# Batches of four adaLN units, gated rows shifted by 64 bytes, and two orders of the split products, in a hybrid decoder step

## The chip, the cores and the metric

One core of a Trainium2 chip. The metric is the device time of one execution in microseconds (us): the median of three runs. The engines are TensorE (PE, with its weight loads as PEld), VectorE (DVE), ScalarE (ACT), GpSimd (POOL) and SyncE (SP, which only issues DMAs here).

## The reference, cut to what matters

One inference step of a two-layer trunk over 512 prompt tokens and 64 sample tokens (576 columns, eight samples of eight tokens), width 1024, float32. Each layer is a half SwiGLU, a mixer, and a second half SwiGLU:

```
cs = silu(c)
for l in range(2):
    mod = cs @ ada_w[l] + ada_b[l]                  # nine blocks of 1024
    sh1, sc1, g1, sh2, sc2, g2, sh3, sc3, g3 = split(mod, 9)
    h = rms_norm(x, g) * (1 + sc1) + sh1
    x = x + 0.5 * g1 * ((silu(h @ w_gate) * (h @ w_up)) @ w_down)   # inner width 2816
    h = rms_norm(x, g) * (1 + sc2) + sh2
    x = x + g2 * mixer(h)            # l = 0: GLA and gMLP heads; l = 1: mLSTM
    ...                              # a second SwiGLU with sh3, sc3, g3
y = rms_norm(x, g) * (1 + scf) + shf
```

So there are four feed-forward sub-layers, called (0,0), (0,1), (1,0) and (1,1) here, in the order (0,0), mixer 0, (0,1), (1,0), mixer 1, (1,1), final norm. The product `cs @ ada_w`, with only nine rows of `cs`, is the adaLN work.

## The kernel before, in words

Activations lie with features on the 128 partitions and the 576 tokens along the row. Every dense product is made in three parts: weights and activations are split into a high part (rounded to fp32r) and a low part (the rest), and PE makes high x high, high x low and low x high (`tile3`). The 576 columns are two halves of 288, whose sums lie in two PSUM banks, so one tile of 128 x 128 weights costs six matmuls of 288 columns: three products times two halves, each with a weight load of its own. `dense` runs eight such tiles (k) into one PSUM buffer: 48 matmuls. `self.turn` picks the order of the six: "products" (both halves of one product, then the next), "halves" (three products of one half, then of the other), "serpent" (the second product's halves the other way round) or "low" (the third product before the second). `ffn` sets one of these for each of the four feed-forwards and "products" everywhere else:

```
self.turn = {(0, 0): "halves", (0, 1): "serpent", (1, 0): "low", (1, 1): "products"}[l, i]
```

A feed-forward works in three groups of 8, 7 and 7 blocks of the inner width. For each block j: a gate product (`pg`), silu on ACT, an up product (`pu`), their product on DVE, and the split of that into `hh` and `hl`, the gated rows. The first gate and up of a sub-layer are made together (`dense_pair`), as the norm hands out its rows k by k. Then eight down products (m) run over the group's `hh` and `hl`: 8 x 8 x 6 = 384 matmuls in the first group, 336 in each other. Group by group, gate and up are 768 matmuls in the first (96 of them the pair) and 672 in each other.

The weights come through SP in units of up to 512 KB (`w_load`, three buffers) and are split by ACT and DVE some three pieces ahead (`w_split`).

The adaLN product is cut into 80 tiles of 128 x 2048 (1 MB each) in ten groups of eight. A "unit" is one step of `ada_gen`: units 0 to 7 of a group issue four matmuls on 32 of PE's columns each (the trace shows eight instructions, as float32 takes two), a ninth step copies the sums to SBUF (`adasb`), a tenth transposes them and makes shift, scale and gate (`mod`). `fill(n)` takes n steps; (0,0) and (0,1) have 20 to take: one behind each gate product and one behind each up product until they are used up. `finish`, at a sub-layer's end, takes one step, the last row sums of squares, and seven more, while the next norm starts on DVE and ACT. `ada_dma` loads tiles up to six ahead into seven buffers.

SBUF is given out by pools, as a stack: a pool that is opened lies above those that are open, and what was closed is used again. Inside a pool, buffers lie in order of first use. `reuse_waits="tile"` lets a new tile wait for the last reader of each old tile whose bytes it takes. In a feed-forward two pools are opened: `room()` is the adaLN pool (`adasb` 2048 bytes a partition, `mod` 576, and seven `adaw` buffers of 8192), `hp` holds `hh`, `hl` (2304 bytes each) and small tiles. In (0,0) `room()` comes first, in the other three `hp`. In (0,1) and (1,0) the first use is of `adasb` and `mod`, then of `adaw`. A pool's first `adaw` tile goes into the lowest buffer; in (1,0) the next ones go from the top downwards; from the eighth tile on the buffers repeat in the same order. The weights `whi` and `wlo` start at multiples of 128 bytes, the normed rows `xh` and `xl` as well. `hh` and `hl` start 64 bytes past such a multiple in (0,0), as 7 x 8192 + 2048 + 576 = 59968 = 468 x 128 + 64, and at a multiple in the other three.

The norm of the next sub-layer opens its pool (`rstd` 2304 bytes, four `yn` buffers of 2304) when both are closed: for (1,0) at the byte where the pools of (0,1) started, for mixer 1 33408 bytes above the byte where those of (1,0) started. In front of some places a `spare` tile keeps `adaw` buffers clear of the next norm.

Of the kernel before, what the change touches and what calls it, by code (L numbers as in the profile page):

```python
# [98 lines left out]
def all_units():  # L99
    yield from ffn_units(0, 0)  # L100
    yield from ab_units()
    yield from ffn_units(0, 1)
    yield from ffn_units(1, 0)
    yield from ml_units()
    yield from ffn_units(1, 1)
# [22 lines left out]
class Trunk:  # L128
    def __init__(self, ctx, tc, ins, outs):
        self.tc, self.nc, self.ins, self.outs = tc, tc.nc, ins, outs  # L130
        pool = lambda name, bufs=1, **kw: ctx.enter_context(tc.tile_pool(name=name, bufs=bufs, **kw))
        self.const = pool("const")
        self.wp = pool("wp", 2)
        self.work = pool("work", 2)
        self.psd = pool("psd", 2, space=PSUM)
        self.psc = pool("psc", 3, space=PSUM)
        self.psa = pool("psa", 1, space=PSUM)
        c = self.const
        self.x = c.tile([P, KD, T], F32, name="x")
        self.sh = c.tile([P, 7, KD, NC], F32, name="sh")  # L140
        self.am = c.tile([P, 7, KD, NC], F32, name="am")
        self.gm = c.tile([P, 6, KD, NC], F32, name="gm")
        self.adab = c.tile([P, 160], F32, name="adab")
        self.gn = c.tile([P, 7, KD], F32, name="gn")
        self.ones = c.tile([P, P], F32, name="ones")
        self.ident = c.tile([P, P], F32, name="ident")
        self.eps = c.tile([P, 1], F32, name="eps")
        self.cs = c.tile([P, KD, 32], F32, name="cs")

        self.units, self.pieces, off = [], [], 0  # L150
        for u, (n, _) in enumerate(all_units()):
            self.units.append((off, n))
            off += P * n
            self.pieces += [(u, c0, min(512, n - c0)) for c0 in range(0, n, 512)]
        self.n_load = self.n_split = self.n_piece = 0
        self.raw, self.split = {}, {}

        self.ada_load = 0
        self.ada_tiles = {}
        self.ada = self.ada_gen()  # L160
        self.ada_done = self.ada_step = 0
        self.ada_ahead = 0
        self.queue = []
        self.cut = HT
        self.turn = "products"


    def w_load(self, upto):
# [30 lines left out]
    def tile3(self, ps, wh, wl, xh, xl, start, stop):  # L199

        mm = self.nc.tensor.matmul
        c = self.cut
        parts = [(slice(512 - c, 512), slice(0, c)), (slice(512, 512 + T - c), slice(c, T))]
        products = ((wh, xh), (wh, xl), (wl, xh))
        turns = {"products": [(j, a) for j in range(3) for a in range(2)],
                 "halves": [(j, a) for a in range(2) for j in range(3)],
                 "serpent": [(0, 0), (0, 1), (1, 1), (1, 0), (2, 0), (2, 1)],
                 "low": [(j, a) for j in (0, 2, 1) for a in range(2)]}[self.turn]
        seen = [0, 0]
        for j, a in turns:  # L210
            w, xx = products[j]
            o, t = parts[a]
            seen[a] += 1
            mm(ps[:w.shape[1], o], w, xx[:, t], start=start and seen[a] == 1, stop=stop and seen[a] == 3)  # L214

    def psum(self):

# [89 lines left out]
    def fill(self, n):  # L307
        for _ in range(n):
            if next(self.ada, 0) == 0:
                return  # L310
            self.ada_step += 1

    def fill_mm(self, n):

        while n and self.ada_step % 10 < 8:
            self.fill(1)
            n -= 1
# [138 lines left out]
    def ffn(self, l, i, ss, fills, gap):  # L456
        nc = self.nc
        left = fills
        s = l * 3 + 2 * i
        if s:  # L460
            self.norm(s, ss, mid=self.split_next)
        else:
            self.first_norm(ss)
        with ExitStack() as ctx:
            room = lambda: self.ada_pool(ctx, f"ada{l}{i}", 7, 8 * gap)
            if s == 0:
                room()
            hp = ctx.enter_context(self.phase(f"hp{l}{i}"))
            if s:
                room()  # L470
            xs = self.xk()
            self.turn = {(0, 0): "halves", (0, 1): "serpent", (1, 0): "low", (1, 1): "products"}[l, i]
            f0 = 0
            for gi, n in enumerate(FGROUPS):
                hh = [hp.tile([P, T], F32R, name=f"hh{j}", tag=f"hh{j}") for j in range(n)]
                hl = [hp.tile([P, T], F32R, name=f"hl{j}", tag=f"hl{j}") for j in range(n)]
                for j in range(n):
                    if gi == 0 and j == 0:
                        pg, pu = self.dense_pair(xs, KS)
                        if self.ada_step % 10 == 8:  # L480
                            self.fill(2)
                        if fills:
                            self.ada_prefetch()
                    else:
                        pg = self.dense(xs, KS)
                    sg = hp.tile([P, T], F32, name="sg", tag="sg", bufs=2)
                    nc.scalar.activation(sg, pg, AF.Silu)  # L487
                    if gi or j:
                        n_fill = min(left, 1)
                        self.fill(n_fill)  # L490
                        left -= n_fill
                        pu = self.dense(xs, KS)
                    h = hp.tile([P, T], F32, name="h", tag="h", bufs=2)
                    nc.vector.tensor_tensor(out=h, in0=sg, in1=pu, op=ALU.mult)  # L494
                    self.hilo(h, hh[j], hl[j])
                    if gi or j:
                        n_fill = min(left, 1)
                        self.fill(n_fill)
                        left -= n_fill
                last = gi == len(FGROUPS) - 1  # L500
                if last:
                    self.log_exp()
                    ss = self.ss_tiles()
                for m in range(KD):
                    ps = self.dense((hh, hl), range(n))
                    if last and m:
                        self.sumsq(m - 1, ss)
                    self.x_add(m, ps, self.gm[:, s])
                    if last and not fills:
                        self.ada_dma(min(self.ada_load + 1, self.ada_stop))  # L510
                f0 += n
            self.turn = "products"
            self.finish(ss)
        return ss

# [1156 lines left out]
```

## Time and profile before

| | |
|---|---|
| median of three runs | 2802.16 us (2801.65 to 2807.85) |
| profiled execution, its time | 2799.31 us |
| its span, first to last instruction | 2797.5 us |
| PE busy | 2722.1 us of the span, 97% |
| PEld, DVE, ACT, POOL busy | 2457.4, 1264.6, 839.3, 193.6 us |
| mean granted PE clock | 0.987 |
| PE in the chain that ended last | 90%, of which 74% is line 214, the matmul of `tile3` |

A row of the timeline gives an instruction's start, how long it took, engine, line, operation, what it writes and reads, its shape, and how many were merged. Matmuls overlap: a 288-column one takes 0.29 us from start to end, but the next starts some 0.13 us after it, so stretches are read from start to start. A row of windows gives the stretch, its length, the busy time and (in brackets) the number of instructions by engine, the granted clock, the mean busy share of the DMA engines, and GB/s.

### The profile page before, as it was taken

Reading aid. Unit: us, or ns where it says so; the run is one execution under the profiler, and the core shown is the slowest. Engines: PE = TensorE matmul, PEld = TensorE weight load, DVE = VectorE, ACT = ScalarE, POOL = GpSimd, SP = SyncE. Lnnn points to the kernel's source line nnn. Section 1 sums busy time; section 2 is a strip of 40 time slices with the busy share of each in tenths; the row PEclk is TensorE's granted clock in tenths of the full one; section 3 lists DMA queues with packets and bytes.
Section 4 is the critical chain, followed back from the end, with each engine's and each line's share of the span. In section 5 each row is a group of like instructions: output and inputs, shape, how many; then the busy total and the mean of one; then the engine's idle time right before and its main releaser. Section 6 shows DMA issues by size and latency. Waiting matters only on the chain.

```text
span 2797.5 us, 45631 instructions
## 1 busy us (share of the span) xinstructions
PE 2722.1 (97%) x19182; PEld 2457.4 (88%) x19182; DVE 1264.6 (45%) x2442; ACT 839.3 (30%) x1508; POOL 193.6 (7%) x263
## 2 busy tenths in 40 slices
PE   6999999999999999999999999999999999999997
PEld 4899999787788999998999997999577667999997
DVE  4233334456552333345333336654766776333334
ACT  4222223332242222234222234334323324222223
POOL 1000000022110000001000004310100111000000
PEclk9999999999799999999999999999999999999999
DMA  7533223221147442223222234467875665222222
GB/s 288 212 126 136 84 82 116 90 77 39 37 168 271 136 138 81 85 84 113 83 84 80 87 126 171 151 179 237 317 280 208 258 250 198 84 83 82 84 76 73
DMA packets 114741, 388.49 MB, mean 139 GB/s; under 512 B 19417, under 2 KB 37097, under 8 KB 95721
## 3 DMA queue, kind: packets, MB, share of 16 engines
q1 hardware_dynamic: 102088, 336.62, 35.7%
q0 software_dynamic: 4880, 35.06, 3.2%
q10 hardware_dynamic: 7568, 13.90, 1.3%
q8 instruction: 151, 2.47, 0.4%
q14 instruction: 54, 0.43, 0.0%
HBM read 324.95 MB, written 60.59 MB: 138 GB/s over the span
## 4 chain that ended last, share of the span: by engine, by line
PE 90%; DVE 4%; ACT 2%; issue 1%; DMA 1%; POOL 1%; SPq 0%; DVEq 0%; ACTq 0%; POOLq 0%
PE psd L214 74%; PE psd L555 2%; PE psc L1509 2%; PE psa L274 1%; PE psc L1397 1%; PE psa L1480 1%; PE psc L1414 1%; PE psc L822 1%; DVE yn L381 1%; POOL qe L805 1%; PE psc L1363 1%; PE psd L1488 1%; DVE xl L371 1%; PE psd L1366 1%; PE psd L1367 0%
## 5 line engine op out<-in xcount | busy, mean ns | idle before, releaser
L214 PE MATMUL psd<-xh,whi 128*128 128x288 f32 x3648 | 852.7, 299 | 11.7 <-ACT xh L382 7.6
L214 PE MATMUL psd<-xl,whi 128*128 128x288 f32 x3648 | 842.9, 297 | 7.9 <-DVE xl L371 7.5
L214 PE MATMUL psd<-xh,wlo 128*128 128x288 f32 x3648 | 839.8, 296 | 1.5 <-DVE wlo L185 1.5
L185 DVE TENSOR_TENSOR wlo<-wraw,whi 128x512 fp32r<-128x512 f32 (+1 forms) x696 | 459.2, 698 | 455.2 <-ACT whi L184 450.9
L214 PEld LDWEIGHTS psd<-xh,whi 128*128 128x128 f32 x3648 | 607.9, 189 | 55.7 <-issue 18.1
L214 PEld LDWEIGHTS psd<-xl,whi 128*128 128x128 f32 x3648 | 608.1, 189 | 13.4 <-DVE xl L371 12.8
L214 PEld LDWEIGHTS psd<-xh,wlo 128*128 128x128 f32 x3648 | 607.7, 189 | 1.8 <-DVE wlo L185 1.8
L184 ACT CAST whi<-wraw 128x512 fp32r<-128x512 f32 (+1 forms) x696 | 400.1, 608 | 416.2 <-PE psd L214 376.0
L214 PE MATMUL psd<-hl,whi 128*128 128x288 f32 x1408 | 329.3, 295 | 0.0
L214 PE MATMUL psd<-hh,whi 128*128 128x288 f32 x1408 | 329.3, 295 | 0.0
L214 PE MATMUL psd<-hh,wlo 128*128 128x288 f32 x1408 | 329.2, 295 | 0.0
L428 DVE SCALAR_TENSOR_TENSOR x<-psd,gm,x 128x512 f32<-128x512 f32 x136 | 102.1, 750 | 355.6 <-PE psd L214 355.6
L214 PEld LDWEIGHTS psd<-hh,whi 128*128 128x128 f32 x1408 | 235.9, 188 | 1.7 <-issue 1.7
L214 PEld LDWEIGHTS psd<-hl,whi 128*128 128x128 f32 x1408 | 235.8, 188 | 0.0
L214 PEld LDWEIGHTS psd<-hh,wlo 128*128 128x128 f32 x1408 | 235.1, 188 | 0.0
L494 DVE TENSOR_TENSOR h<-sg,psd 128x576 f32<-128x576 f32 x88 | 66.4, 754 | 349.2 <-PE psd L214 349.2
L420 ACT CAST hh<-h 128x576 fp32r<-128x576 f32 x88 | 59.4, 675 | 488.4 <-DVE h L494 488.4
L487 ACT ACTIVATE sg<-psd 128x576 f32<-128x576 f32 x88 | 57.4, 652 | 359.4 <-PE psd L214 359.3
L367 POOL TENSOR_TENSOR yn<-x,rstd 128x576 f32<-128x576 f32 x30 | 49.3, 1651 | 1062.5 <-ACT rstd L395 1005.9
L214 PE MATMUL psd<-hz,whi 128*128 128x288 f32 x512 | 95.8, 309 | 0.9 <-DVE kc L1301 0.9
L421 DVE TENSOR_TENSOR hl<-h,hh 128x576 fp32r<-128x576 f32 x88 | 66.8, 759 | 65.2 <-ACT hh L420 65.2
L1492 DVE SCALAR_TENSOR_TENSOR cu<-cu,wd,psd 128x512 f32<-128x512 f32 x128 | 87.0, 742 | 13.5 <-PE psd L1488 13.5
(331 smaller groups left out, 2244.4 us busy)
## 6 DMA issues: line engine op xcount, KB each, us to landing
wraw<-wall SPq DMA_DIRECT2D x284, 512.0 KB, 3.6
adaw<-ada SPq DMA_DIRECT2D x80, 1024.0 KB, 7.6
cu<-mC SPq DMA_DIRECT2D x32, 1024.0 KB, 6.5
Cs<-cu POOLq DMA_DIRECT2D x32, 1024.0 KB, 6.7
wraw<-wall SPq DMA_DIRECT2D x64, 448.0 KB, 3.3
szp<-zp SPq DMA_DIRECT2D x32, 256.0 KB, 2.6
bx<-sx SPq DMA_DIRECT2D x16, 512.0 KB, 6.1
zt<-szp SPq DMA_DIRECT2D x16, 512.0 KB, 8.0
```

The lines of the kernel that those rows point to most:

```text
L184: nc.scalar.copy(hi[:, :n], raw)
L185: nc.vector.tensor_tensor(out=lo[:, :n], in0=raw, in1=hi[:, :n].bitcast(F32), op=ALU.subtract)
L214: mm(ps[:w.shape[1], o], w, xx[:, t], start=start and seen[a] == 1, stop=stop and seen[a] == 3)
L367: eng.tensor_tensor(out=y, in0=self.x[:, k, :], in1=rstd, op=ALU.mult)
L420: self.nc.scalar.copy(hi, y)
L421: self.nc.vector.tensor_tensor(out=lo, in0=y, in1=hi.bitcast(F32), op=ALU.subtract)
L428: nc.vector.scalar_tensor_tensor(out=xp, in0=ps[:, :TP], scalar=g[:, m, 0:1], in1=xp, op0=ALU.mult, op1=ALU.add)
L487: nc.scalar.activation(sg, pg, AF.Silu)
L494: nc.vector.tensor_tensor(out=h, in0=sg, in1=pu, op=ALU.mult)
L555: mm(ps[i], xx[:, k, self.tokens(i)], w, start=k == 0 and j == 0, stop=k == KD - 1 and j == 2)
L1492: nc.vector.scalar_tensor_tensor(out=cu[:, g], in0=cu[:, g], scalar=dec, in1=pu[:, i], op0=ALU.mult, op1=ALU.add)
L1509: mm(pc, self.v[:, s, g * P:(g + 1) * P], self.wk[:, s], start=s == 0, stop=s == 3)
```

## The change

- `tile3` has two orders left: "there and back" where `self.there` is true (this is "serpent": the second product takes the halves the other way round), else "products". `there` is true outside of the feed-forwards. In them it is true for gate and up of the first group, and of a later group as long as adaLN steps are left to take when the group starts; it is false for all down products.
- Steps are taken behind the up product only, by `fill_some`: up to four units in a row, not past the eighth of a group; the copy and the transposes alone.
- `room()` comes ahead of `hp` in all four feed-forwards.

```
-        products = ((wh, xh), (wh, xl), (wl, xh))
-        turns = {"products": [(j, a) for j in range(3) for a in range(2)],
-                 "halves": [(j, a) for a in range(2) for j in range(3)],
-                 "serpent": [(0, 0), (0, 1), (1, 1), (1, 0), (2, 0), (2, 1)],
-                 "low": [(j, a) for j in (0, 2, 1) for a in range(2)]}[self.turn]
-        seen = [0, 0]
-        for j, a in turns:
-            ...
+        for j, (w, xx) in enumerate(((wh, xh), (wh, xl), (wl, xh))):
+            for o, t in parts[::-1] if self.there and j == 1 else parts:
+                mm(ps[:w.shape[1], o], w, xx[:, t], start=start and j == 0, stop=stop and j == 2)
...
+    def fill_some(self, left):
+
+        at = self.ada_step % 10
+        n = min(left, 1 if at >= 8 else min(4, 8 - at))
+        self.fill(n)
+        return n
...
-            if s == 0:
-                room()
+            room()
             hp = ctx.enter_context(self.phase(f"hp{l}{i}"))
-            if s:
-                room()
             xs = self.xk()
-            self.turn = {(0, 0): "halves", (0, 1): "serpent", (1, 0): "low", (1, 1): "products"}[l, i]
...
+                self.there = gi == 0 or left > 0
...
                     if gi or j:
-                        n_fill = min(left, 1)
-                        self.fill(n_fill)
-                        left -= n_fill
                         pu = self.dense(xs, KS)
...
                     if gi or j:
-                        n_fill = min(left, 1)
-                        self.fill(n_fill)
-                        left -= n_fill
+                        left -= self.fill_some(left)
+                self.there = False
...
-            self.turn = "products"
+            self.there = True
             self.finish(ss)
```

More of the change, by code (lines that the diff above doesn't have):

```diff
@@ L203, in tile3 @@
         parts = [(slice(512 - c, 512), slice(0, c)), (slice(512, 512 + T - c), slice(c, T))]
-        products = ((wh, xh), (wh, xl), (wl, xh))
-        turns = {"products": [(j, a) for j in range(3) for a in range(2)],
-                 "halves": [(j, a) for a in range(2) for j in range(3)],
-                 "serpent": [(0, 0), (0, 1), (1, 1), (1, 0), (2, 0), (2, 1)],
-                 "low": [(j, a) for j in (0, 2, 1) for a in range(2)]}[self.turn]
-        seen = [0, 0]
-        for j, a in turns:
[L211 to L214, printed above, removed]
+        for j, (w, xx) in enumerate(((wh, xh), (wh, xl), (wl, xh))):
+            for o, t in parts[::-1] if self.there and j == 1 else parts:
+                mm(ps[:w.shape[1], o], w, xx[:, t], start=start and j == 0, stop=stop and j == 2)
     def psum(self):
@@ L511, in ffn @@
                 f0 += n
-            self.turn = "products"
+            self.there = True
             self.finish(ss)
```

## The prediction

> **What bounds the kernel now.** I read the page first: shares of the engines and the chain that ended last.
>
> ```profile
> span 2797.5 us, 45631 instructions
> PE 2722.1 (97%) x19182; PEld 2457.4 (88%) x19182; DVE 1264.6 (45%) x2442; ACT 839.3 (30%) x1508; POOL 193.6 (7%) x263
> PE 90%; DVE 4%; ACT 2%; issue 1%; DMA 1%; POOL 1%; SPq 0%; DVEq 0%; ACTq 0%; POOLq 0%
> ```
>
> PE is the bound nearly everywhere; the other 10% of the chain lies mostly at the seams between sub-layers. So the change is worth (1) what it saves on PE inside the stages and (2) what it does to the seams. For (1) I read PE's timeline at the borders of stages without adaLN work. The four feed-forwards run the four orders, so the trace of before already compares them. Each trio is: first gate/up matmul of the third group, first down matmul, first matmul behind the downs.
>
> ```profile
> 349.21 0.30 PE L214 MATMUL psd<-xh,whi 128*128 128x288 f32 x1
> 438.81 0.29 PE L214 MATMUL psd<-hh,whi 128*128 128x288 f32 x1
> 483.23 1.13 PE L343 MATMUL psc<-sqa,ones 128*128 128x288 f32 x4
> ...
> 1133.21 0.43 PE L214 MATMUL psd<-xh,whi 128*128 128x288 f32 x2
> 1221.69 0.29 PE L214 MATMUL psd<-hh,whi 128*128 128x288 f32 x1
> 1265.93 1.13 PE L343 MATMUL psc<-sqa,ones 128*128 128x288 f32 x4
> ...
> 1568.12 0.43 PE L214 MATMUL psd<-xh,whi 128*128 128x288 f32 x2
> 1657.72 0.43 PE L214 MATMUL psd<-hh,whi 128*128 128x288 f32 x2
> 1702.52 0.41 PE L343 MATMUL psc<-sqa,ones 128*128 128x288 f32 x1
> ...
> 2645.71 0.29 PE L214 MATMUL psd<-xh,whi 128*128 128x288 f32 x1
> 2735.31 0.29 PE L214 MATMUL psd<-hh,whi 128*128 128x288 f32 x1
> 2780.11 0.65 PE L343 MATMUL psc<-sqa,ones 128*128 128x288 f32 x2
> ```
>
> The gate/up group (672 matmuls) takes 89.60 us in (0,0) "halves", 88.48 in (0,1) "serpent", 89.60 in (1,0) "low", 89.60 in (1,1) "products": 133.3 ns a matmul, but 131.7 for there-and-back. The down group (336) takes 44.42, 44.24, 44.80 and 44.80. So order alone is worth 1.12 us per 672, and "halves", which gains nothing in gate/up, gains 0.38 us per 336 in (0,0)'s downs, the only rows that start 64 bytes off: that is the offset's worth in that order.
>
> **The change part by part.**
>
> (a) Four units in a row. One lone unit between two dense products, and the seven in a row of a `finish`:
>
> ```profile
> 61.33 0.29 PE L214 MATMUL psd<-xh,wlo 128*128 128x288 f32 x1
> 61.55 1.07 PE L274 MATMUL psa<-adaw,cs 128*32 128x512 f32 x8
> 62.55 0.40 PE L214 MATMUL psd<-xh,whi 128*128 128x288 f32 x1
> ...
> 1266.99 1.06 PE L274 MATMUL psa<-adaw,cs 128*32 128x512 f32 x8
> 1269.27 6.21 PE L274 MATMUL psa<-adaw,cs 128*32 128x512 f32 x56
> ```
>
> Lone: 62.55 - 61.33 = 1.22 us from matmul to matmul in place of 0.13, so 1.09 each, 4.35 for four. In a row each further unit costs (6.21 - 1.06) / 6 = 0.86. Four together: 1.22 + 3 x 0.86 - 0.13 = 3.66. Saved: 0.69 per four. (0,0) starts at step 10 and (0,1) at 50, both take 20 steps as 4, 4, 1, 1, 4, 4, 1, 1: eight batches, **-5.5 us**. Copy and transposes stay alone, as before. The instructions are the same in number, their DMAs too; the tiles' loads only come in bursts (last rival). Eight slots are used, seven in group one and the eighth in group two, so in (0,0) and (0,1) `there` is true in groups one and two.
>
> (b) Order in gate/up. (0,0) halves to there-and-back in two groups: -2.24 (in the first group 768 - 96 = 672 count, as the pair waits for the norm). (1,0) and (1,1): -1.12 each in group one; their other groups stay at 133.3. (0,1) loses there-and-back in group three: +1.12. Sum **-3.4**.
>
> (c) Order in the mixers, "products" to there-and-back, 1.67 ns a matmul. Mixer 1's input: 30 dense products behind the pair, 1440 matmuls, -2.4. Mixer 0: six output products and four for the gate, 480 matmuls, -0.8. Another 384 there and 768 in mixer 1's heads are threaded between other matmuls, where the order hardly repeats; bounds 0 and -1.9, I take half. Sum **-4.2**, between -3.2 and -5.1.
>
> (d) Downs: "products" on rows 64 bytes off, which the trace doesn't have. Nearest rows per 336: same order without offset 44.80, same offset in another order 44.42. I take 44.42, the row with the offset itself. A sub-layer has 1056 downs, 3.14 times the 336: (0,0) 0; (0,1) loses there-and-back, 44.42 - 44.24 = 0.18, +0.6; (1,0) and (1,1) -0.38 x 3.14 = -1.2 each. Sum **-1.8**. Bounds: 44.80 gives +1.2 + 1.8 = +3.0; if a new order could gain both reliefs (0.38 and 0.56, 43.86) it is -8.9.
>
> (e) The seams, where the moved `room()` has a price. With `hp` first, the next norm took over bytes of gated rows, long read. With the adaLN pool first it takes over `adaw` buffers, which `finish` still reads.
>
> ```profile
> 1268.89 0.99 ACT L394 ACTIVATE rstd<-psc,eps 128x288 f32<-128x288 f32 x2 [0.84 <-PE psc L343]
> 1270.63 2.65 DVE L367 TENSOR_TENSOR yn<-x,rstd 128x576 f32<-128x576 f32 x2 [3.35 <-ACT rstd L395]
> 1276.91 0.53 PE L214 MATMUL psd<-xh,whi 128*128 128x288 f32 x2 [1.43 <-ACT xh L382]
> ...
> 1705.48 0.99 ACT L394 ACTIVATE rstd<-psc,eps 128x288 f32<-128x288 f32 x2 [0.84 <-PE psc L343]
> 1705.86 5.36 PE L274 MATMUL psa<-adaw,cs 128*32 128x512 f32 x48
> 1712.18 1.07 PE L274 MATMUL psa<-adaw,cs 128*32 128x512 f32 x8 [0.96 <-DMA adaw<-ada]
> 1713.50 0.53 PE L214 MATMUL psd<-xh,whi 128*128 128x288 f32 x2 [0.26 <-ACT xh L382]
> ```
>
> (0,1) to (1,0): bytes 0 to 2624 of the pool are `adasb` and `mod`, the lowest `adaw` buffer is 2624 to 10816. `rstd` (0 to 2304) is free, but the first three `yn` (2304 to 9216) lie in that buffer, the fourth partly. (0,1) has units 40 to 63 in seven buffers, the lowest holds 40, 47, 54 and 61. Unit 61 is the fifth of the seven in a row: it ends at 1269.27 + 1.06 + 4 x 0.86 = 1273.8. So `yn` on DVE (and on POOL) starts at 1273.8 instead of 1270.63; behind it on DVE stand the next weights' low parts and the small steps that the first `xh` needs. The whole norm is **3.2 us** later, PE's first matmul at 1280.1. (1,0) to mixer 1: `rstd` lies at 33408 to 35712, in the fourth buffer from below (27200 to 35392) and the fifth. Counted from the top down these hold units 68 and 67. Unit 68, fourth in a row, ends at 1705.86 + 1.06 + 3 x 0.86 = 1709.5, so `rstd` starts **4.1 us** later than 1705.48, and the chain behind it on ACT and DVE as well. `mlw` on POOL's queue waits for unit 69 (1710.4) with POOL's `yn` behind it, which needs `rstd` (ready at 1711.3) anyway. The other seams keep what they had: mixer 0's norm lies above both pools, and neither (0,0)'s order nor the final norm's place changes.
>
> PE then stands idle for 4.6 and 4.3 us (1275.5 to 1280.1, 1713.25 to 1717.6). The clock may halve behind that, as it did behind the idle stretch of 3.06 us at 33.4:
>
> ```profile
> 36.48 0.61 PE L214 MATMUL psd<-xh,whi 128*128 128x288 f32 x1 [3.06 <-ACT xh L382]
> ...
> 26.00:36.00 10.00, 5.08 (x28) 0.87 (x28) 3.54 (x13) 2.19 (x4) 0.00 (x0) 0.83 0.90 349
> 36.50:46.00 9.50, 8.35 (x32) 7.68 (x33) 8.21 (x14) 6.40 (x10) 2.83 (x2) 0.50 0.25 78
> ...
> 1276.19 0.67 ACT L382 CAST xh<-yn 128x576 fp32r<-128x576 f32 x1 [3.85 <-DVE yn L381]
> 1288.76 0.67 ACT L382 CAST xh<-yn 128x576 fp32r<-128x576 f32 x1
> ```
>
> The norm hands out a row each 12.57 / 7 = 1.8 us, and PE needs 12 x 0.133 = 1.6 for it, twice that at half clock; some 7 us of half clock is mostly made up behind the last rows. I count 1.0 for both seams, bounds 0 and 5. Sum of (e) **+8.3**, bounds 0 (no such wait) and +12.
>
> **Sum.** -5.5 - 3.4 - 4.2 - 1.8 + 8.3 = -6.6 us on the profiled execution of 2799.31 us (2797.5 span, 1.8 around it), which becomes 2792.7. The median of the runs is 2802.16, 2.9 above the profiled one; the prediction is 2802.16 - 6.6 = **2795.6**. A measurement of this kernel can tell some 0.3% (8.4 us) from no change, so I stand just short of "faster".
>
> **The rivals.**
>
> - The seams cost nothing: the waits of (e) don't arise, because buffers fall elsewhere than I count. For it: the kernel keeps `spare` tiles against this elsewhere. Against it: the pool sizes. -14.9, 2787.3. Chance 0.18.
> - Offset and order work together: products off by 64 gain 0.94 per 336. -8.9 in place of -1.8: 2788.5. For it: each relief shows alone. Against it: no row shows two together. Chance 0.16.
> - The offset does nothing for this order; downs run at 44.80. -6.6 + 4.8: 2800.4. For it: that the offset helps is shown for one order only. Chance 0.12. The Trainium skill, TensorE: Matmul & The Clock Gate, section "Step-by-step: what each phase is for", speaks for this one: PE has two independent read ports, and loading the next weights doesn't take from the moving rows, so where rows lie against weights shouldn't matter. The trace disagrees in one order: 44.42 against 44.80.
> - Slower: the batch outruns its tiles. A batch takes four 1 MB tiles within 3.7 us; the next is due two dense products later.
>
> ```profile
> 60.00:65.00 5.00, 5.00 (x39) 3.99 (x38) 1.29 (x2) 1.68 (x3) 0.00 (x0) 1.00 1.00 416
> 65.00:70.00 5.00, 5.00 (x40) 4.12 (x38) 0.75 (x1) 0.00 (x0) 0.00 (x0) 1.00 1.02 429
> ```
>
> At full queues 416 GB/s move. From batch to batch 12.7 + 3.7 = 16.4 us, 6.8 MB, for four tiles and two weight units of 512 KB, 5.2 MB: it fits, with three tiles in hand. If each of the eight batches nevertheless stood still for 2 us or more, the sum is +9.4: 2811.6. Below 1.9 us a batch it isn't slower by 0.3%. Chance 0.04.
>
> **How the numbers follow.** My forecast has 0.50, spread over 2791 to 2800 by the bounds of (c) and (e). The range takes in the first three rivals: 2787 to 2801. Faster by over 0.3% (below 2793.8): the first two rivals and a quarter of the forecast's own spread, 0.18 + 0.16 + 0.13 = 0.47. Slower 0.05. Same: the rest, 0.48.
>
> **What would show it.** Batches of 32 on `psa` with 3.7 us of PE each, eight of them. Gate/up of (0,1)'s third group at 89.6 and of (0,0)'s second at 88.5 plus its fill. Downs per 336: 44.4 in all four; 44.8 or 43.9 is a rival. At (1,0)'s start `yn` on DVE waiting for the adaLN matmul of line 274, at mixer 1's start `rstd` on ACT waiting for the same; PE idle over 4 us at both, and perhaps a granted clock below 1. It is wrong if those waits are absent, or if PE waits for `adaw` inside (0,0) or (0,1).

## The result, and the profile after

The change makes the kernel faster by about half a per cent: medians 2802.47 us before and 2791.5 us after (five runs each, 2787.19 to 2793.75 after); the ratio over the runs timed side by side is 0.9949 [0.9938, 0.996]. The forecast was 2795.6. The total lies close to it, but its parts do not: the feed-forwards gained twice what the sum gave them, and the profiled execution gave much of that back in a place that the change does not slow.

From the page of the kernel after:

```profile
span 2789.7 us, 45643 instructions
PE 2709.7 (97%) x19182; PEld 2449.5 (88%) x19182; DVE 1264.5 (45%) x2442; ACT 839.1 (30%) x1508; POOL 193.4 (7%) x263
PE 90%; DVE 4%; DMA 2%; ACT 1%; issue 1%; POOL 1%; DVEq 0%; SPq 0%; ACTq 0%; POOLq 0%
```

PE has the same 19182 matmuls and is 12.4 us less busy; its share of the chain is unchanged. The matmul of `tile3` is L206 now, the adaLN matmul L266. PE's timeline at the borders of stages, as before: the third groups of (0,0) and (0,1), then the second and third of (1,0).

```profile
343.89 0.42 PE L206 MATMUL psd<-xh,whi 128*128 128x288 f32 x2
431.26 0.42 PE L206 MATMUL psd<-hh,whi 128*128 128x288 f32 x2
475.68 0.65 PE L342 MATMUL psc<-sqa,ones 128*128 128x288 f32 x2
...
1122.64 0.42 PE L206 MATMUL psd<-xh,whi 128*128 128x288 f32 x2
1210.00 0.42 PE L206 MATMUL psd<-hh,whi 128*128 128x288 f32 x2
1254.42 0.65 PE L342 MATMUL psc<-sqa,ones 128*128 128x288 f32 x2
...
1424.05 0.42 PE L206 MATMUL psd<-xh,whi 128*128 128x288 f32 x2
1511.41 0.42 PE L206 MATMUL psd<-hh,whi 128*128 128x288 f32 x2
1555.83 0.43 PE L206 MATMUL psd<-xh,whi 128*128 128x288 f32 x2
1645.42 0.42 PE L206 MATMUL psd<-hh,whi 128*128 128x288 f32 x2
1689.84 1.14 PE L342 MATMUL psc<-sqa,ones 128*128 128x288 f32 x4
```

The downs take 475.68 - 431.26 = 44.42 in (0,0) and the same in the others. But the groups in the order of products take **87.36** us in (0,0) and (0,1) and in the second group of (1,0): 130.0 ns a matmul, a rate that no row of before has. The third group of (1,0), same order and same size, takes 89.59: 133.3 ns. (1,1) repeats (1,0).

A batch of four units, and the two seams, in the timelines of PE, DVE and ACT:

```profile
67.93 0.43 PE L206 MATMUL psd<-xh,wlo 128*128 128x288 f32 x2
68.29 3.64 PE L266 MATMUL psa<-adaw,cs 128*32 128x512 f32 x32
71.86 0.53 PE L206 MATMUL psd<-xh,whi 128*128 128x288 f32 x2
...
1257.76 6.21 PE L266 MATMUL psa<-adaw,cs 128*32 128x512 f32 x56
1262.39 2.64 DVE L366 TENSOR_TENSOR yn<-x,rstd 128x576 f32<-128x576 f32 x2 [6.62 <-PE psa L266]
1268.64 0.85 PE L206 MATMUL psd<-xh,whi 128*128 128x288 f32 x2 [4.66 <-ACT xh L381]
...
1693.18 6.21 PE L266 MATMUL psa<-adaw,cs 128*32 128x512 f32 x56
1696.89 0.89 ACT L393 ACTIVATE rstd<-psc,eps 128x288 f32<-128x288 f32 x2 [4.93 <-PE psa L266]
1704.86 0.85 PE L206 MATMUL psd<-xh,whi 128*128 128x288 f32 x2 [5.46 <-ACT xh L381]
```

The 10 us behind PE's restart at each seam, as windows: length, busy time of PE, PEld, DVE, ACT and POOL with their instructions, then the granted clock, the DMA share and GB/s.

```profile
1268.50:1278.50 10.00, 9.15 (x52) 8.39 (x53) 9.67 (x17) 7.32 (x12) 4.29 (x3) 0.83 0.17 52
1704.50:1714.50 10.00, 9.15 (x51) 8.47 (x51) 9.48 (x15) 7.30 (x12) 4.31 (x4) 0.78 0.17 52
```

Both waits are where the prediction put them: `yn` on DVE and `rstd` on ACT wait for the adaLN matmul. Their times name the unit as well: with 1.06 us for the first unit in a row and 0.86 for each further one, the fifth of the seven that start at 1257.76 ends at 1262.3 (`yn` starts at 1262.39), and the fourth of the seven that start at 1693.18 ends at 1696.8 (`rstd` starts at 1696.89). From the last down matmul to the next sub-layer's first matmul it is 1268.64 - 1254.42 = 14.22 us (before 1276.91 - 1265.93 = 10.98) and 1704.86 - 1689.84 = 15.02 (before 10.99).

By the same kind of borders, the two profiled executions compare so (us; each sub-layer from its first dense matmul to behind its last down):

| stage | before | after | difference | the sum had |
|---|---|---|---|---|
| (0,0) | 446.75 | 438.46 | -8.3 | -5.0 |
| (0,1) | 440.89 | 436.44 | -4.5 | -1.0 |
| (1,0) | 425.61 | 421.20 | -4.4 | -2.3 |
| (1,1) | 425.79 | 421.20 | -4.6 | -2.3 |
| the two seams | 21.97 | 29.24 | +7.3 | +8.3 |
| mixer 0 with its seams | 341.81 | 342.31 | +0.5 | } |
| mixer 1, input | 228.13 | 226.12 | -2.0 | } -4.2 |
| mixer 1, heads | 375.71 | 383.40 | **+7.7** | } |
| mixer 1, output | 36.97 | 36.73 | -0.2 | } |
| start | 36.48 | 37.22 | +0.7 | 0 |
| span | 2797.5 | 2789.7 | -7.8 | -6.6 |

Three things ask for an experiment: the seams, the new rate of 130.0 ns, and the heads.

### The profile page after: what moved, and what is told of

Its sections match the earlier page's. It is cut to its first block, busy times and chain, and to the rows that moved or that the text cites. A ratio compares the mean times of both kernels' runs of the same rounds, so it can differ in the third digit from the quotient of the medians.

```text
span 2789.7 us, 45643 instructions
## 1 busy us (share of the span) xinstructions
PE 2709.7 (97%) x19182; PEld 2449.5 (88%) x19182; DVE 1264.5 (45%) x2442; ACT 839.1 (30%) x1508; POOL 193.4 (7%) x263
## 4 chain that ended last, share of the span: by engine, by line
PE 90%; DVE 4%; DMA 2%; ACT 1%; issue 1%; POOL 1%; DVEq 0%; SPq 0%; ACTq 0%; POOLq 0%
PE psd L206 73%; PE psa L266 2%; PE psd L547 2%; PE psc L1501 2%; PE psc L1389 1%; PE psa L1472 1%; PE psc L814 1%; PE psc L1406 1%; DVE yn L380 1%; DMA adaw<-ada 1%; POOL qe L797 1%; PE psc L1355 1%; DMA cu<-mC 1%; DVE xl L370 1%; PE psd L1358 1%
## 5 line engine op out<-in xcount | busy, mean ns | idle before, releaser
L206 PE MATMUL psd<-xh,whi 128*128 128x288 f32 x3648 | 789.0, 298 | 19.6 <-ACT xh L381 15.5
L206 PE MATMUL psd<-xl,whi 128*128 128x288 f32 x3648 | 781.1, 295 | 5.8 <-DVE xl L370 5.5
L206 PE MATMUL psd<-xh,wlo 128*128 128x288 f32 x3648 | 779.3, 295 | 1.5 <-DVE wlo L185 1.5
L206 PEld LDWEIGHTS psd<-xh,whi 128*128 128x128 f32 x3648 | 587.8, 189 | 45.0 <-ACT xh L381 19.5
L206 PEld LDWEIGHTS psd<-xl,whi 128*128 128x128 f32 x3648 | 586.5, 189 | 10.6 <-DVE xl L370 9.9
L206 PEld LDWEIGHTS psd<-xh,wlo 128*128 128x128 f32 x3648 | 583.8, 189 | 1.8 <-DVE wlo L185 1.8
L206 PE MATMUL psd<-hh,whi 128*128 128x288 f32 x1408 | 300.5, 294 | 0.0
L206 PE MATMUL psd<-hh,wlo 128*128 128x288 f32 x1408 | 300.4, 294 | 0.0
L206 PE MATMUL psd<-hl,whi 128*128 128x288 f32 x1408 | 299.2, 293 | 0.0
L206 PEld LDWEIGHTS psd<-hh,whi 128*128 128x128 f32 x1408 | 225.8, 188 | 0.0
L206 PEld LDWEIGHTS psd<-hl,whi 128*128 128x128 f32 x1408 | 225.8, 187 | 0.0
L206 PEld LDWEIGHTS psd<-hh,wlo 128*128 128x128 f32 x1408 | 224.9, 188 | 0.0
L206 PE MATMUL psd<-hz,whi 128*128 128x288 f32 x512 | 94.0, 305 | 1.1 <-DVE kc L1293 1.1
L1484 DVE SCALAR_TENSOR_TENSOR cu<-cu,wd,psd 128x512 f32<-128x512 f32 x128 | 87.1, 743 | 15.6 <-PE psd L1480 15.6
```

Source lines behind the costliest of these rows:

```text
L206: mm(ps[:w.shape[1], o], w, xx[:, t], start=start and j == 0, stop=stop and j == 2)
L1484: nc.vector.scalar_tensor_tensor(out=cu[:, g], in0=cu[:, g], scalar=dec, in1=pu[:, i], op0=ALU.mult, op1=ALU.add)
```

## The experiments

**The seams alone.** The gated rows go back ahead of the adaLN pool, as before, and a pad of 64 bytes keeps them off:

```
-            room()
+            if s == 0:
+                room()
             hp = ctx.enter_context(self.phase(f"hp{l}{i}"))
+            if s:
+                hp.tile([P, 16], F32, name="pad")
+                room()
```

> The changed kernel, but in (0,1), (1,0) and (1,1) the gated rows' pool comes first again, with an unused tile of 64 bytes at its foot, so that the rows still start 64 bytes off and the next norm again takes bytes of gated rows. Seam theory (the norm waits for adaLN buffers): the first matmul of (1,0) comes 1.4 us behind the last adaLN matmul instead of 4.7, that of mixer 1 under 0.5 us instead of 5.5; the stretch from the last down product to the next first matmul is 11.0 us at both, as before the change, in place of 14.2 and 15.0: 7.3 us less, and up to 2 more where the clock no longer halves. Rival (the stretches are longer for another reason, such as the rows' new place in memory for ACT and DVE): both stay over 14 us. Downs stay at 44.4 us per 336.

Measured: median 2784.76 us (6 runs; before 2804.04), ratio 0.9926 [0.9912, 0.9939]. Its PE, DVE and ACT timelines at the two places:

```profile
1256.25 1.14 PE L342 MATMUL psc<-sqa,ones 128*128 128x288 f32 x4
1260.94 2.65 DVE L366 TENSOR_TENSOR yn<-x,rstd 128x576 f32<-128x576 f32 x2 [3.35 <-ACT rstd L394]
1267.23 0.53 PE L206 MATMUL psd<-xh,whi 128*128 128x288 f32 x2 [1.43 <-ACT xh L381]
...
1689.62 1.14 PE L342 MATMUL psc<-sqa,ones 128*128 128x288 f32 x4
1692.58 0.98 ACT L393 ACTIVATE rstd<-psc,eps 128x288 f32<-128x288 f32 x2 [0.84 <-PE psc L342]
1700.61 0.53 PE L206 MATMUL psd<-xh,whi 128*128 128x288 f32 x2 [0.58 <-ACT xh L381]
```

10.98 and 10.99 us again, and `yn` and `rstd` wait for the norm's own chain. So the price of the moved `room()` is shown: 3.24 + 4.03 = 7.27 us. The downs stay at 44.42: the offset needs no price. What was not lost, as far as it can be read, is the 1.0 counted for the clock: although the clock fell to one half at both seams (0.83 and 0.78 above), the first group of (1,0) took 104.64 in the changed kernel and 105.83 here, and mixer 1's input 226.12 and 226.18. The first group also has two values of its own (104.6 and 105.8, in identical code), so a loss below about 1 us can't be read there. Nor does the half clock belong to the longer seams alone: it followed the short first seam too in three of the runs below, those with single units, with products in the mixers and with the changed end of the second group (0.83 over the first 10 us of (1,0), 1.00 here).

**Order, all there-and-back in gate/up.** `self.there = gi == 0 or left > 0` becomes `self.there = True`.

> The changed kernel with there-and-back in every gate/up group, products in the downs. All six gate/up groups that ran in the order of products then take 88.5 us per 672 if a group's order alone sets its rate: four lose 1.1 each (87.4 to 88.5), two gain 1.1 (89.6 to 88.5), 2.2 us more in sum. If what goes ahead sets the rate, some there-and-back groups leave 88.5 too.

Measured: 2799.18 us in one run. Third groups of (0,0) and (0,1) and second and third of (1,0) and (1,1): all 89.6 us, 133.3 ns. There-and-back, which ran at 131.7 in (0,1) before, doesn't run so in these groups. In the second group of (0,0) it does: a product of 48 matmuls there takes 6.40 us (133.3 ns each) ahead of the adaLN transposes and 6.32 (131.7) behind them, with the same order throughout. An order has no rate of its own.

**Order, second group there-and-back, third in products.** `self.there = gi < 2`.

> The changed kernel with there-and-back in the first two gate/up groups of every feed-forward and products in the third alone; it differs from the changed one in the second groups of (1,0) and (1,1). State theory (a products group runs at 130.0 ns a matmul behind a there-and-back group and its offset downs, at 133.3 behind another products group): the third groups of (1,0) and (1,1) take 87.4 us instead of 89.6, the second ones 88.5 instead of 87.4; 1.1 us less for each feed-forward. Rival (the third group of these two is slow for its place): 89.6 stays in the third group, 1.1 us more for each.

Measured: 2788.81 us in one run. (1,0), from the second group on:

```profile
1424.58 0.42 PE L206 MATMUL psd<-xh,whi 128*128 128x288 f32 x2
1514.18 0.42 PE L206 MATMUL psd<-hh,whi 128*128 128x288 f32 x2
1558.60 0.42 PE L206 MATMUL psd<-xh,whi 128*128 128x288 f32 x2
1645.97 0.42 PE L206 MATMUL psd<-hh,whi 128*128 128x288 f32 x2
```

There-and-back takes 89.60 in the second group, and now the third group, slow in the changed kernel, runs at 87.37 with the same instructions on the same bytes: what went ahead decides.

**No offset.** As the first experiment, without the pad.

> The changed kernel, but with the gated rows' pool first in (0,1), (1,0) and (1,1) and no tile at its foot: the rows start at a multiple of 128 bytes there, as before the change; (0,0) keeps its offset. Downs by products then take 44.8 us per 336 there instead of 44.4, 3.6 us more in sum, and the seams lose their 7.3. If the offset downs are what leaves PE in the state for 130.0 ns, the products groups of (0,1), (1,0) and (1,1) all take 89.6, 6.7 us more; if there-and-back ahead is enough, three of them stay at 87.4.

Measured: 2793.3 us in one run. Second group, downs, third group of (1,0):

```profile
1424.81 0.42 PE L206 MATMUL psd<-xh,whi 128*128 128x288 f32 x2
1514.41 0.42 PE L206 MATMUL psd<-hh,whi 128*128 128x288 f32 x2
1559.21 0.42 PE L206 MATMUL psd<-xh,whi 128*128 128x288 f32 x2
1648.81 0.42 PE L206 MATMUL psd<-hh,whi 128*128 128x288 f32 x2
```

Downs 44.80, products 89.60 in both groups and in (0,1)'s third; (0,0), whose rows are still off by 64, keeps 87.36. The offset is thus worth 0.38 per 336 downs and, unforeseen, 2.24 in each of the three gate/up groups that ran at 87.36 with it, whose own rows it doesn't touch.

**Which rows ahead set the rate.** On the first experiment's kernel, one insertion in each sub-layer:

```
+ once = gi == 2 and ((l, i, j) in ((1, 1, 0), (0, 0, 3)))   # this gate product there-and-back
+ self.there = self.there or once
  pg = self.dense(xs, KS)
...
- self.there = False                                          # the downs
+ self.there = (l, i) == (0, 1) or (l, i, gi) == (1, 0, 1)
```

> Built on e1_pad. Three insertions, each read in its own sub-layer. (1,1): in the third gate/up group only the first dense product (48 of 672 matmuls) goes there-and-back, the rest in the order of products. (1,0): the downs of the second group (336) go there-and-back, nothing else changes. (0,1): all downs go there-and-back. (0,0), a control the other way: in its third group, which runs at 87.36 us, the fourth gate product alone goes there-and-back. Theory (the same order has two lasting rates, 130.0 and 133.3 ns, and what went through PE just before picks one; there-and-back leads into the fast one): (1,1) third group 87.4 to 87.6 instead of 89.60; (1,0) third group 87.4 as well, its second downs 44.2 to 44.8; (0,0) third group stays within 0.2 us of 87.36. Rival 1 (the rate alternates from group to group, or hangs on the gate/up group before, and a few matmuls don't matter): both third groups stay at 89.6. Rival 2 (any break of the pattern resets it at random): (0,0) goes up toward 89 us too. If the offset and there-and-back could both gain on downs, as one rival of the prediction has it, (0,1) has downs of 43.9 per 336 instead of 44.42; if not, 44.2 to 44.8. Total against e1_pad: -4.4 by the theory, 0 by rival 1.

Measured: 2789.05 us in one run. The theory that any there-and-back just ahead leads into the quicker rate fell. (0,0)'s third group, and (1,0) from its second downs on:

```profile
343.96 0.42 PE L206 MATMUL psd<-xh,whi 128*128 128x288 f32 x2
432.60 0.43 PE L206 MATMUL psd<-hh,whi 128*128 128x288 f32 x2
...
1516.37 0.43 PE L206 MATMUL psd<-hh,whi 128*128 128x288 f32 x2
1561.53 0.43 PE L206 MATMUL psd<-xh,whi 128*128 128x288 f32 x2
1651.13 0.42 PE L206 MATMUL psd<-hh,whi 128*128 128x288 f32 x2
```

A there-and-back product put into a group at the quicker rate ends it: (0,0)'s six products ahead run at 130.0 ns, those behind at 133.3, 88.64 in all. Put at the head of the slow group, in (1,1), it doesn't help (89.52). Downs there-and-back on offset rows are dearer, not cheaper: 45.16 per 336 in (1,0), 44.80 and 45.16 in (0,1). The group behind them in (1,0) stays at 89.60, and the third group of (0,1), which ran at 87.36 behind offset downs in products, takes 89.58 here. So the rival of the prediction in which offset and order add is excluded.

**What the downs follow.** On the first experiment's kernel, only the end of the second group goes there-and-back: `self.there = True` ahead of the seventh up product in (1,0), ahead of the seventh gate product in (1,1).

> e1_pad with the end of the second gate/up group there-and-back in two sub-layers: in (1,0) the last dense product of the group (the seventh up, 48 matmuls), in (1,1) the last two (seventh gate and up, 96); the rest of that group, the downs and the third group stay in the order of products. Theory (what the downs follow decides: downs behind there-and-back hand on the fast rate, downs behind products at 130.0 hand on the slow one): third groups of (1,0) and (1,1) at 87.36 us instead of 89.59, second groups 87.4 to 87.7; total -4 us against e1_pad, about 2781 us. Rival (the whole group before must have gone there-and-back, or the rate turns over from group to group whatever comes between): third groups stay at 89.59, total within 0.5 us of e1_pad beside the scatter of the heads.

Measured: median **2778.3** us (5 runs; before 2805.41), ratio 0.9906 [0.9889, 0.9923], the lowest median of all versions, though the interval overlaps that of the first experiment (0.9912 to 0.9939). The traces show it more clearly. (1,0), end of the second group to the end of the third:

```profile
1508.31 0.42 PE L206 MATMUL psd<-hh,whi 128*128 128x288 f32 x2
1552.73 0.42 PE L206 MATMUL psd<-xh,whi 128*128 128x288 f32 x2
1640.10 0.42 PE L206 MATMUL psd<-hh,whi 128*128 128x288 f32 x2
```

87.37 in place of 89.59, in (1,1) as well; the second groups take 87.52 and 87.68. So 48 matmuls ahead of the downs decide the rate of the 672 behind them. A short there-and-back passage worked here through offset downs; directly ahead of the products (the insertion in (1,1) above) it didn't.

**Other pads.** Pads of 32, 128 and 192 bytes in (0,1), (1,0) and (1,1).

> e1_pad with other sizes of the pad: 32 bytes in (0,1), 128 in (1,0), 192 in (1,1), instead of 64 in all three; (0,0) keeps its 64. Theory (what counts is whether the gated rows start 64 bytes off a multiple of 128): (1,1) as with 64, downs 44.42, second group 87.36; (1,0) as without a pad, downs 44.80, second and third group 89.60; (0,1) with 32 bytes lies somewhere between 44.42 and 44.80 or at one of them, its third group 87.36 or 89.60 to match. Rival (any pad does, since it is the place in the pool that counts): all at 44.42. Total within 5 us of e1_pad.

Measured: 2783.45 us in one run. With 32 and with 128 bytes the downs take 44.80 and the products 89.6; with 192 the downs take 44.42. So among the four offsets tried, the two that lie 64 off a multiple of 128 gain, the other two don't. The groups of (1,1) came out the other way round, however:

```profile
2498.47 0.43 PE L206 MATMUL psd<-xh,whi 128*128 128x288 f32 x2
2588.05 0.42 PE L206 MATMUL psd<-hh,whi 128*128 128x288 f32 x2
2632.47 0.42 PE L206 MATMUL psd<-xh,whi 128*128 128x288 f32 x2
2719.83 0.42 PE L206 MATMUL psd<-hh,whi 128*128 128x288 f32 x2
```

Second group 89.58 behind a there-and-back group, third 87.36 behind a slow products group. With the runs above: behind downs that run in products on rows 64 off, a group in products was fast where the group ahead ended there-and-back or in slow products, and slow where it ended in fast products, with this one second group as the exception. So this is a summary of these runs, not a rule. The starts of single matmuls in the changed kernel's trace show how the two rates differ: in the fast second group of (1,0) they are 128 and 132 ns apart in turn, while in the slow third group three of four are 130 to 132 ns apart and every fourth 140. What the chip holds from one group to the next stays open.

**Units one by one.** The first experiment's kernel with the units at the old places, `n_fill = min(left, 1)` between gate and up and again behind the gated row.

> e1_pad with the adaLN units back one by one, two chances for each pair of products as before the change; all else as e1_pad. By the prediction's term (a), (0,0) and (0,1) take 5.5 us more together, 2.7 each, in their first two groups (first about +1 to +1.5, second about +1.2 to +1.7; in the second group the order of two states may add or hide up to 1.1). The profile's window of (0,0) should show lone units of about 1.2 us from matmul to matmul. Rival: a unit costs the same alone and in a row, and what the first two groups gained came from the order; then (0,0) and (0,1) stay within 0.5 us. Total against e1_pad +5.5 or 0, with some 4 us of scatter from the heads.

Measured: 2795.27 us in one run. (0,0)'s first two groups take 215.35 us with single units and 211.51 with batches, +3.8; (0,1)'s 214.08 and 210.73, +3.4. First groups have two or more values here too: (0,1)'s two groups take 209.47 in the changed kernel, against which single units cost +4.6. Two units in a row in (0,0):

```profile
61.07 1.06 PE L266 MATMUL psa<-adaw,cs 128*32 128x512 f32 x8
68.59 1.06 PE L266 MATMUL psa<-adaw,cs 128*32 128x512 f32 x8
```

7.52 us for a unit and 48 matmuls; less 1.09 for the unit that is 134.0 ns a matmul, against 131.7 for a product with no unit beside it (6.32 us, in the same group). So a unit also slows the dense product behind it by 0.11 us, and batches cut the number of such products from 32 to 8. That is a part of the gain that term (a) lacked; how large, the scatter of the first groups leaves open by about 1 us.

**Products in the mixers.** The first experiment's kernel with `self.there = False` outside the feed-forwards.

> e1_pad with the order of products in both mixers instead of there-and-back, feed-forwards as in e1_pad. By the prediction's term (c), +4.2 us (3.2 to 5.1) against e1_pad: mixer 1's input +2.4 (226.2 to 228.5), mixer 0 +0.8 to +1.5, heads up to +1. Rival A: the order does nothing in the mixers, where other matmuls break the pattern; every stage stays within 0.4. Rival B: there-and-back itself costs the heads the 4 to 7 us that they show above the profile of the kernel before (379.6 to 383.4 against 375.7); then the heads fall to about 376 and the total falls by 2 to 5 us. If the heads' extra time is the granted clock's, they stay between 376 and 384 with as many spells of clock 0.5 as there are microseconds over 375.

Measured: median 2789.12 us (5 runs; before 2806.22), ratio 0.9933 [0.992, 0.9947], not to be told from the first experiment's 0.9926. In the trace mixer 1's input takes 228.07 (+1.9), mixer 0 342.12 (-0.8), the heads 385.12. So there-and-back isn't what makes the heads longer than the 375.7 of the first profile of before. Only the input shows its term: in all profiles it takes 226.05 to 226.79 with there-and-back and 228.07 to 228.13 with products.

**The kernel before once more**, for its profile.

> The kernel before once more, for its profile alone: is the 375.71 us of the heads in the first profile usual for it? Theory (the spells of clock 0.5 in the heads come and go from execution to execution, and the first profile of the kernel before happened to hold none): this one shows heads of 377 to 384 us with spells of 3.4 us at clock 0.5, and a span some 2 to 6 us over 2797.5. Rival (the change slows the heads): heads at 375.7 again, no spells. All other stages as in the first profile, within 1 us.

Measured: 2807.04 us, span 2805.3. The heads as windows: the kernel before in its first profile, the same once more, the kernel after, and the kernel with other pads (the seventh number is the granted clock).

```profile
1941.63:2317.35 375.72, 370.41 (x2092) 244.11 (x2090) 254.83 (x548) 122.36 (x281) 40.97 (x66) 1.00 0.72 266
```

```profile
1940.79:2325.09 384.30, 378.52 (x2092) 246.47 (x2090) 254.86 (x548) 122.27 (x281) 40.90 (x66) 0.97 0.71 260
```

```profile
1930.97:2314.37 383.40, 377.95 (x2091) 246.19 (x2090) 254.80 (x548) 122.30 (x281) 40.89 (x66) 0.97 0.71 260
```

```profile
1928.98:2305.18 376.20, 371.80 (x2092) 243.92 (x2090) 254.80 (x548) 122.35 (x281) 40.93 (x66) 0.99 0.71 265
```

The unchanged kernel spans both values, 375.7 at a clock of 1.00 and 384.3 at 0.97, and so does the new code. In the traces the granted clock falls to 0.5 for 3.4 us once in the first of these windows, six times in the second and in the third, and twice in the last. A spell of 3.4 us at half clock does the work of 1.7 us, so five more spells make 8.5 us, by this estimate, of the 8.6 between the two profiles of the unchanged kernel. The +7.7 of the table is the clock's scatter, not the change's. Why the spells come in one execution and not in another stays open. All other stages of the second profile lie within 1.4 us of the first's. Against it the changed kernel's span is 15.6 us shorter, against the first 7.8; the ratio of the timed runs, 0.9949, is about -14 us of some 2804.

## Why the prediction came out as it did

- **(a), four units in a row, -5.5.** Right in its working: 71.86 - 68.06 (the second matmul of the row at 67.93) = 3.80 from matmul to matmul, eight batches of 32. Undersized: undone, it costs 3.8 + 3.4 = 7.2 us (one run each way, 8.4 against (0,1) of the changed kernel). Missing was the slowdown of the dense product behind each interruption, 24 x 0.11 = 2.6 by this estimate.
- **(b), order in gate/up, -3.4.** The step failed at its premise that there-and-back is always 131.7 ns and products always 133.3. Both have 133.3 as well as a faster rate, 131.7 and 130.0, and offset downs ahead can hand on either. Four groups (third of (0,0) and (0,1), second of (1,0) and (1,1)) ran at 87.36 where the sum had 89.60: -9.0 us that it lacked.
- **(c), order in the mixers, -4.2.** The input's -2.4 was measured as -2.0 and, undone, +1.9 (1.3 to 2.1 over all profiles). The rest (-1.8) isn't seen: mixer 0 took 342.87 us in the first experiment and 339.59 in the one with other pads, with the same code for it, and the heads move by 8.6 us with the clock.
- **(d), downs, -1.8.** Right: 44.42 in all four sub-layers. The rivals that would have made it 44.80 or 43.9 are excluded. The Trainium skill, TensorE: Matmul & The Clock Gate, section "Step-by-step: what each phase is for", has two independent read ports. From these the prediction argued that the place of the rows should make no difference; 44.42 against 44.80 with the pad alone changed says that it does.
- **(e), seams, +8.3.** Right in place, tile and engine, and +3.24 and +4.03 against 3.2 and 4.1. The clock fell to one half at both, as the prediction thought it might, but it did so at the short first seam of three other runs as well, and the 1.0 for it doesn't show.
- **The total.** The sum lacked 9.0 us of (b) and about 2 of (a), and counted some 2 us of gain too many in (c) and 1 of loss too many in (e): with the terms as measured it is -6.6 - 9.0 - 2 + 2 - 1 = -16.6, close to the -15.6 between the changed kernel and the second profile of before. The runs gave -11 by the medians and -14 by the ratio; the rest lies within their scatter (2801.65 to 2808.94 before, 2787.19 to 2793.75 after) and wasn't traced. So the forecast of -6.6 had the right sign and the right seams, but only about half of the size by the ratio. It had stood just short of a gain clear of 0.3%, with 0.48 for that and 0.47 for more, and the runs show more. That the time came within 4.1 us of the forecast (2791.5 against 2795.6) is partly luck: the heads of the changed kernel ran at the lower clock in its profiled execution, which is also its median, and hid some 7 us of a gain that the sum hadn't counted. At which clock the heads ran in the other executions of the result wasn't traced.

## What to carry to other kernels

When a pool is moved to shift an address, look up which tiles of the next stage inherit its bytes: a pad of 64 bytes kept the gain of the shift and saved the 7.3 us at the seams. A rate read from one stage holds for that stage with what runs ahead of it; before it is used elsewhere, look for the same instructions at another rate. And before stages of two profiles are compared, set the granted clock beside each: here one stage of unchanged code moved by 8.6 us, more than the change's whole prediction.

## What the runs showed of the hardware that was not expected

- Matmuls of the same order, size and bytes run steadily at 130.0 or 133.3 ns over 672 matmuls, and what ran ahead decides which: 48 matmuls in another order ahead of 336 downs switch it (87.36 and 89.59 us), downs in products on rows without the offset are followed by 89.60, and one product of another order within a group at 130.0 ends it. The spacing is 128 and 132 ns in turn at the quicker rate, and 130 to 132 with every fourth 140 at the slower one. There-and-back has 131.7 and 133.3.
- Moving rows 64 bytes off a multiple of 128 take 132.2 ns a matmul in the order of products against 133.3 in the downs, but 133.3 to 134.4 there-and-back, where unshifted rows took 131.7 (44.24 us per 336 in (0,1) before).
- PE stood still for 4.66 us at the first seam and 5.46 us at the second, and the granted clock was 0.5 for 3.4 us from the restart at the first, and for 6.8 us at the second, from 2.7 us before the restart (0.83 and 0.78 over the 10 us shown). It cost nothing that can be read; DVE, which takes part in making the rows, was busy for 9.67 and 9.48 of these 10 us, which may be why. The Trainium skill, TensorE: Matmul & The Clock Gate, section "What's actually happening", has the clock halve after an idle window of about 3.4 us. Here the clock fell at the end of the first stand but 2.8 us into the second, so the figure is met only roughly, and the length of a stand doesn't settle it alone: behind the first seam of 10.98 us, where PE idles 1.43 us at the end, the clock is 1.00 in the first experiment (the window from 1267 to 1277 us) and 0.83 in the run with products in the mixers (1267.2 to 1277.2).
